# Small products of a chunked delta rule, issued in another order

## Chip, cores, metric

The kernel runs on one core of one Trainium2 chip. The metric is the device time of one execution in microseconds (us), the median over runs. Engines are named as the profile names them: PE is TensorE's matmul side, PEld its weight loads, DVE VectorE, ACT ScalarE, POOL GpSimd, SP SyncE, which issues the DMAs.

## What is computed

A token sequence `x` of 256 tokens of 1024 channels goes through two hybrid layers (latent attention, gated convolution, sparse attention, feed-forward), then through a second block with two branches, differential attention and a gated delta rule in both directions over time, and at last through a mixture of 16384 small experts. Only the delta rule matters here. The reference states it as a recursion over tokens: a state S of 64 x 64 for each of 16 heads and for each direction, which every token decays, corrects along its key and adds to, and which is read with the token's r. It first runs over 256 context tokens, which leave only their state, and from that state over the 256 tokens of `x`, which also give outputs.

The kernel computes the same by chunks of 32 tokens: within a chunk the products of all pairs and a triangular inverse, between chunks a recursion over 8 chunks.

## The kernel before

**Staging.** The program has three parts: the hybrid layers (0 to about 1050 us in the profile), the second block (to about 2070 us), and the experts. In the second block weight products (lines 325 to 327 and 343 to 345, f32 split in two parts of one pass each), the attention's heads and the delta rule are separate streams that share the engines. The delta rule is worked off in four rounds: source 0 (context) for heads 0 to 7, then for heads 8 to 15, source 1 (`x`) for both. A round is a call of `wkv_front`, all that needs no state, and one of `wkv_back`, the recursion over chunks and, for source 1, the outputs. The large tiles of a round ("w8", nine buffers) are needed by the next one, so that a front can do only part of its work before the recursion ahead of it has ended.

**Order.** Dependences and the order in which each engine's queue is filled come from a planner that lays out the whole traced program against a simulated time (line 1920). The delta rule is traced under high priority (lines 1546 and 1550), so the planner puts other streams' work into its gaps. On the chip each engine works its queue in order. The planner treats a tile's reads and writes by their place in the free dimension: a product into other partitions of the same columns of a bank still waits for an earlier read of them. Banks: the stream of the fronts has two that rotate, the stream of the recursions three.

**Names.** `d` is the direction (0 forward, 1 backward), `m` one of four channel tiles, `b` one of the two heads in it (rows 0 to 63 or 64 to 127), `q` one of four pairs of chunks, `c2` the chunk in it. In step n of the recursion direction 0 works on chunk n and direction 1 on chunk 7 - n.

- Line 1270, in `wkv_front`: pair products of every chunk, 64 rows by 64 columns of the array. Rows by `b`, columns by `c2`. Lines 1272 and 1274 mask them on DVE (two multiplies per bank without outputs, four with).
- Lines 1290 to 1294: the triangular inverse, 31 steps of a multiply and a subtraction on DVE. Lines 1315 and 1322 work beside it.
- Line 1344, in `wkv_back`: WR times the state S. Rows by `b`, columns by `c2` (with source 0 only 32 columns). Line 1347 adds the result to U on DVE, line 1353 copies outputs on ACT.
- Line 1359: the inverse ML times U, 32 rows by 32 columns of the array, both by `c2`. Line 1360 evicts it (ACT).
- Line 1369: KT times U, rows by `c2`, columns by `b`. Lines 1370 and 1371 update S on DVE.
- Line 1384: the outputs, 64 rows by `c2`, 32 columns by the chunk in its token tile, `g`. Lines 1385 and 1386 sum them up on DVE.
- Line 996 belongs to another stream: 128 rows, four strips of 32 columns in turn. Line 260 is the helper that evicts on ACT; lines 263, 266 and 269 are the helpers for multiply, add and subtract.

Of the kernel before, what the change touches and what calls it, by code (L numbers as in the profile page):

```python
# [19 lines left out]
T = 256  # L20
# [6 lines left out]
# ---------------------------------------------------------------- host layout  # L27
# [56 lines left out]
def constants():  # L84
    p = Pack()
    pos = np.arange(256)
    c, s = _rope_tab(pos, 16, 32)
    p.add("mla_c", _tok(c)), p.add("mla_s", _tok(s))
    c, s = _rope_tab(pos, 8, 16)
# [6 lines left out]
    # second block  # L96
# [5 lines left out]
    h = np.arange(128) // 64  # L102
# [91 lines left out]
# ---------------------------------------------------------------- device  # L194
class Kern:
# [17 lines left out]
    # tiles  # L213
# [22 lines left out]
    @contextmanager  # L236
    def stream(self, sfx, single=False):
        """tiles of small operands and banks of their own for one of the streams that run side by side"""
        old = self.sfx, self.single
        self.sfx, self.single = sfx, single  # L240
        yield
        self.sfx, self.single = old
# [7 lines left out]
    # engines  # L250
# [20 lines left out]
    def rsqrt(self, x, n):  # L271
        """x: tile AP [p, n]; returns 1/sqrt(x), bit estimate and three Newton steps."""
# [14 lines left out]
    # weights  # L287
# [21 lines left out]
    def pieces(self, name, piece=None):  # L309
        """Yields (h, l) pieces of a weight unit."""  # L310
# [9 lines left out]
    def mmA(self, ps, wh, wl, xh, xl, first, last):  # L320
        """ps[m, t] += W^T X; wh/wl [128, nk, 128], xh/xl [128, nk, t]"""
# [7 lines left out]
    @contextmanager  # L329
    def behind(self, ins):  # L330
        """queues products behind an earlier one"""
        if ins is None:
            yield
        else:
            with self.tc.issue_after(ins.ins):
                yield

    def mmB(self, ps, xh, xl, wh, wl, first, last):
        """ps[t, n] += X^T W for one token tile; xh/xl [128, nk, 128], wh/wl [128, nk, n]"""
# [7 lines left out]
    def linB_unit(self, name, hh, hl, n):  # L347
        """token-major product with a K=1024 unit of n columns; one bank [128, 2 token tiles, n]"""
# [12 lines left out]
    def linA_unit(self, name, hh, hl, nk):  # L361
        """channel-major product with a unit [m, k, 128]; yields banks of two m-tiles"""
# [16 lines left out]
    def pairs_split(self, h, lo, ps, scale=None, bias=None):  # L379
        """h + lo = ps (times a per-partition scale)"""  # L380
# [13 lines left out]
    def normT(self, x, g, hh, hl, eps=1e-6, bias=None, spare="", hold=False):  # L394
        """hh + hl = (rms_norm(x) * g [+ bias])^T, x: two token tiles [128, 1024]; with hold the next weights are split behind it"""
# [43 lines left out]
    def softmax(self, ps, p, G, scale, gate=None):  # L439
        """p = softmax(scale * ps) over the last axis (times gate); ps, p [128, G, n] views"""  # L440
# [16 lines left out]
    def rope_rows(self, v, c, s, half, tmp):  # L457
        """v [..., 2*half] in place; c = [cos, cos], s = [-sin, sin] broadcast to the shape of v"""
# [5 lines left out]
    # ------------------------------------------------------------ hybrid layer  # L464
    def layer(self, l, pool):
# [19 lines left out]
        # ---- MLA projections  # L485
# [36 lines left out]
        with self.stream("n", True):  # L522
            # ---- compression
# [68 lines left out]
        # ---- gated convolution  # L592
# [42 lines left out]
        with self.stream("t"):  # L635
            # per-head norms
# [28 lines left out]
        # ---- NSA projections  # L665
# [31 lines left out]
        with self.stream("t"):  # L697
            # attention
# [38 lines left out]
        with self.stream("n"):  # L737
            # ---- compressed branch
# [37 lines left out]
            # ---- selected and window branches  # L776
# [103 lines left out]
        # ---- feed-forward  # L880
# [30 lines left out]
    def gates(self, l, pool, i, hh, hl, park=False):  # L911
        """tanh of half the mixing logits of branch i, two tiles [128, 4, T]"""
# [13 lines left out]
    def merge(self, l, pool, P, M, i, name, TGs, xh, xl):  # L926
        """M (+)= 2 sigmoid(gate i) * (X @ W_o [+ b])"""
# [17 lines left out]
    def in_turn(self, late):  # L945
        """products (t, n, k, operands) in the order of their banks"""
# [7 lines left out]
    def linB_acc(self, name, pw, xh, xl, first, last):  # L954
        """pw[t] [128, 2, 512] += X^T W over two k-tiles of a [2, 1024] unit; the last unit ends one bank after the other"""
# [16 lines left out]
    # ------------------------------------------------------------ second block  # L972
# [5 lines left out]
    def mods_stream(self):  # L978
        """modT [128, 48, 2]: the 6 modulation vectors, channel-major, for x and for ctx; yields after each weight unit"""
# [33 lines left out]
    def mod_rows(self, i, w, out):  # L1013
        """out: two halves [128, 512]: modulation vector i on every partition"""
# [14 lines left out]
    def da_front(self, pool, a, name, hh, hl):  # L1029
        """head maps to a [128, 2, 16, 64]; returns their norms"""  # L1030
# [12 lines left out]
    def da_tail(self, pool, front, g, rope, dst, off):  # L1043
        """normed (and roped) head maps, transposed, to dst [128, 8, *] from column off; yields after every two heads"""
# [29 lines left out]
    def rope_tables(self, pool, g, name):  # L1074
        """[128, (cos, sin), 2 token tiles, 64]: the axial angles with the head gains g [128, 64] folded in"""
# [16 lines left out]
    def shifted(self, out, ps, mt):  # L1092
        """centred shift of one channel tile, psum [128, T] -> out"""
# [6 lines left out]
    def ctx_norm(self, pool, tag):  # L1100
        """the normalised context, in the place of the last layer's activations"""
# [7 lines left out]
    def w_proj(self, pool, src, hh, hl):  # L1109
        """(tanh(wd) | ad) and sigmoid(gd)"""  # L1110
# [14 lines left out]
    def z_proj(self, pool, src, hh, hl, zd):  # L1125
        """shifted r, k, v to zd [128, 24, T]"""
# [19 lines left out]
    def wkv_front(self, pool, src, hf, zd, wa, own=False):  # L1146
        """gated delta rule over one source and 8 heads, both directions, chunks of 32: all that does not need the state.
        Rows of packed token tiles are (c4, t32); rows of stacked ones (c2, (k, b), t32) or (c2, (v, u), t32)."""
# [10 lines left out]
        # normalised keys  # L1159
# [19 lines left out]
        # values by token, packed and in the rows of the stacked tiles  # L1179
# [8 lines left out]
        # bonus  # L1188
# [10 lines left out]
        # decays and products, channel-major  # L1199
# [11 lines left out]
        for d in range(2):  # L1211
            # log decays, chunks of 33 with a leading zero; L: their sums
# [31 lines left out]
            # K: half the inverse decay; b = 2 a kk, k = 2 k_eff  # L1244
# [12 lines left out]
        # pair products by (k, b) in rows, the b rows of the strict ones transposed for the first direction  # L1257
# [4 lines left out]
        for q in range(4):  # L1262
            for b in range(2):
                Q = slice(64 * b, 64 * b + 64)
# [659 lines left out]
```

## Time and profile before

| | us |
|---|---|
| median of three runs | 2906.81 |
| lowest, highest | 2900.73, 2912.28 |
| span of the profiled execution | 2922.4 |
| PE busy in it | 2777.9 (95%) |
| DVE busy | 1985.9 (68%) |
| ACT busy | 1428.5 (49%) |

The profile gives the profiled execution's span, from its first to its last instruction; what lies around it is not told apart. The span is 15.6 us above the median of the runs. In the timeline a row merges neighbours of one line: its length runs from the first start to the last end, and the number in brackets is the idle time of that engine before it, with what ended it. Matmuls are pipelined, so a row's length holds the last product's latency once.

### The profile page before, as it was taken

Reading aid. Unit: us, or ns where it says so; the run is one execution under the profiler, and the core shown is the slowest. Engines: PE = TensorE matmul, PEld = TensorE weight load, DVE = VectorE, ACT = ScalarE, POOL = GpSimd, SP = SyncE. Lnnn points to the kernel's source line nnn. Section 1 sums busy time; section 2 is a strip of 40 time slices with the busy share of each in tenths; the row PEclk is TensorE's granted clock in tenths of the full one; section 3 lists DMA queues with packets and bytes.
Section 4 is the critical chain, followed back from the end, with each engine's and each line's share of the span. In section 5 each row is a group of like instructions: output and inputs, shape, how many; then the busy total and the mean of one; then the engine's idle time right before and its main releaser. Section 6 shows DMA issues by size and latency. Waiting matters only on the chain. (4 is left out here: it accounts for less than half of the span.)

```text
span 2922.4 us, 55072 instructions
## 1 busy us (share of the span) xinstructions
PE 2777.9 (95%) x21880; PEld 2448.0 (84%) x21880; DVE 1985.9 (68%) x4104; ACT 1428.5 (49%) x2417; POOL 13.3 (0%) x36
## 2 busy tenths in 40 slices
PE   7999999999999998999898899898989999999999
PEld 7986688898678997889787678798989998888887
DVE  5986555698665577886868665347787775666665
ACT  4554444555454456564444544225435654444444
POOL 0000000000000000000000000000000000000000
PEclk9999999999899998999888765579999999999999
DMA  5543755454375554544434212045455345666665
GB/s 184 174 143 132 277 196 187 162 177 142 112 249 188 186 192 131 167 145 120 149 120 136 82 34 81 1 137 195 153 174 167 118 139 182 218 214 216 214 214 186
DMA packets 214738, 467.16 MB, mean 160 GB/s; under 512 B 53072, under 2 KB 86608, under 8 KB 213968
## 3 DMA queue, kind: packets, MB, share of 16 engines
q1 hardware_dynamic: 214480, 463.64, 48.5%
q8 instruction: 172, 2.82, 0.4%
q14 instruction: 86, 0.70, 0.1%
HBM read 425.54 MB, written 38.01 MB: 159 GB/s over the span
## 5 line engine op out<-in xcount | busy, mean ns | idle before, releaser
L304 ACT ACTIVATE wh<-raw 128x1024 fp32r<-128x1024 f32 (+2 forms) x726 | 643.6, 890 | 727.5 <-PE a L326 340.3
L269 DVE TENSOR_TENSOR wl<-raw,wh 128x1024 fp32r<-128x1024 f32 (+2 forms) x726 | 732.8, 1012 | 384.6 <-ACT wh L304 374.3
L325 PE MATMUL a<-hh,wh 128*128 128x256 f32 x2784 | 796.6, 286 | 17.6 <-ACT wh L304 10.4
L327 PE MATMUL a<-hh,wl 128*128 128x256 f32 x2784 | 796.6, 287 | 6.8 <-DVE wl L269 6.6
L326 PE MATMUL a<-hl,wh 128*128 128x256 f32 x2784 | 795.1, 286 | 2.5 <-DVE hl L269 1.8
L325 PEld LDWEIGHTS a<-hh,wh 128*128 128x128 f32 x2784 | 534.2, 192 | 29.3 <-ACT wh L304 13.2
L327 PEld LDWEIGHTS a<-hh,wl 128*128 128x128 f32 x2784 | 532.8, 192 | 17.1 <-DVE wl L269 10.9
L326 PEld LDWEIGHTS a<-hl,wh 128*128 128x128 f32 x2784 | 532.9, 191 | 9.7 <-DVE hl L269 2.6
L344 PE MATMUL a<-wl,hh 128*128 128x256 f32 (+2 forms) x640 | 196.4, 307 | 13.6 <-DVE wl L269 13.2
L344 PE MATMUL b<-wl,ah 128*128 128x512 f32 x512 | 200.9, 392 | 0.0
L343 PE MATMUL a<-wh,hh 128*128 128x256 f32 (+2 forms) x640 | 193.1, 306 | 7.5 <-DVE hl L387 6.7
L343 PE MATMUL b<-wh,ah 128*128 128x512 f32 x512 | 191.0, 393 | 3.6 <-issue 3.6
L345 PE MATMUL b<-wh,al 128*128 128x512 f32 x512 | 192.0, 392 | 0.0
L345 PE MATMUL a<-wh,hl 128*128 128x256 f32 (+2 forms) x640 | 191.9, 301 | 0.0
L260 ACT ACTIVATE w<-a 32x512 f32<-32x512 f32 (+1 forms) x168 | 99.4, 592 | 140.2 <-PE a L1359 68.4
L344 PEld LDWEIGHTS a<-wl,hh 128*128 128x128 f32 x640 | 127.3, 199 | 26.2 <-DVE wl L269 16.8
L343 PEld LDWEIGHTS a<-wh,hh 128*128 128x128 f32 x640 | 127.7, 200 | 14.7 <-DVE hl L387 7.3
L1769 ACT ACTIVATE ah<-pact 128x256 fp32r<-128x256 f32 x128 | 52.7, 412 | 169.1 <-PE b L344 163.5
L345 PEld LDWEIGHTS a<-wh,hl 128*128 128x128 f32 x640 | 127.0, 198 | 3.8 <-issue 0.8
L269 DVE TENSOR_TENSOR wl<-rawv,wh 128x1024 fp32r<-128x1024 f32 x84 | 101.8, 1223 | 38.7 <-ACT wh L304 38.6
L827 DVE SCALAR_TENSOR_TENSOR z<-U,pk,z 128x256 f32<-128x256 f32 x240 | 114.6, 477 | 0.8
L269 DVE TENSOR_TENSOR al<-pact,ah 128x256 fp32r<-128x256 f32 x128 | 53.0, 422 | 90.8 <-ACT ah L1769 90.8
(515 smaller groups left out, 4606.4 us busy)
## 6 DMA issues: line engine op xcount, KB each, us to landing
raw<-in_flat SPq DMA_DIRECT2D x266, 512.0 KB, 3.7
raw<-in_peer SPq DMA_DIRECT2D x172, 512.0 KB, 3.9
raw<-in_flat SPq DMA_DIRECT2D x276, 256.0 KB, 3.4
rawv<-in_peer SPq DMA_DIRECT2D x84, 512.0 KB, 4.3
TG<-in_flat SPq DMA_DIRECT2D x28, 512.0 KB, 5.8
qk<-in_flat SPq DMA_DIRECT2D x24, 512.0 KB, 5.2
parked<-act SPq DMA_DIRECT2D x89, 128.0 KB, 1.9
pact<-parked SPq DMA_DIRECT2D x89, 128.0 KB, 4.0
```

The costliest lines, as they stand in the source:

```text
L260: nc.scalar.activation(out, in_, AF.Copy, scale=1.0 if scale is None else scale)
L269: self.nc.vector.tensor_tensor(out, a, b, op=ALU.subtract)
L304: self.nc.scalar.activation(h, src, AF.Copy)
L325: mm(ps, wh[:, k], xh[:, k], start=first and k == 0, stop=False)
L326: mm(ps, wh[:, k], xl[:, k], start=False, stop=False)
L327: mm(ps, wl[:, k], xh[:, k], start=False, stop=last and k == nk - 1)
L343: mm(ps, xh[:, k], wh[:, k], start=first and k == 0, stop=False)
L344: mm(ps, xh[:, k], wl[:, k], start=False, stop=False)
L345: self.last = mm(ps, xl[:, k], wh[:, k], start=False, stop=last and k == nk - 1)
L827: nc.vector.scalar_tensor_tensor(cv[:, c], U[:, c, k_:k_ + T], wd[:, k_:k_ + 1], cv[:, c], op0=ALU.mult, op1=ALU.add)
L1769: nc.scalar.activation(ah, act, AF.Copy)
```

## The change

Five loops are put in another order. No operation is added or taken away and no operand changes; banks that were taken one by one are taken together (`pq`, `pk`).

- Line 1270: both banks of a chunk pair are taken first, `b` goes inside `m`, the masks of both banks come after all products of the pair.
- Line 1344: `m` goes outermost, then `d`, then `b`; the sums of both directions come after all products.
- Line 1359: `m`, `b`, then `d` innermost; both evictions come after all products.
- Line 1369: the same as line 1344, with one bank per direction; the updates of S follow.
- Line 1384: `g` goes from outermost to innermost.

The rest of the diff takes out comments and docstrings. Its core:

```diff
         for q in range(4):
-            for b in range(2):
-                Q = slice(64 * b, 64 * b + 64)
-                ps = self.bank()[:, 0:256 * (1 + src)].rearrange("p (d m x s) -> p d m x s", d=2, m=4, s=32)
-                for d in range(2):
-                    for m in range(4):
+            pq = [self.bank()[:, 0:256 * (1 + src)].rearrange("p (d m x s) -> p d m x s", d=2, m=4, s=32) for b in range(2)]
+            for d in range(2):
+                for m in range(4):
+                    for b in range(2):
+                        Q = slice(64 * b, 64 * b + 64)
                         for c2 in range(2):
...
+            for b in range(2):
                 for d in range(2):
-                    self.mul(ML[:, d, q, b], ps[:, d, :, src], strict[:, 1 - d].unsqueeze(1).to_broadcast([128, 4, 32]))
+                    self.mul(ML[:, d, q, b], pq[b][:, d, :, src], strict[:, 1 - d].unsqueeze(1).to_broadcast([128, 4, 32]))
...
-            for d, q, c2 in dc:
-                rows = slice(64 * c2, 64 * c2 + 64) if src else slice(64 * c2 + 32, 64 * c2 + 64)
-                for m in range(4):
+
+            for m in range(4):
+                for d, q, c2 in dc:
+                    rows = slice(64 * c2, 64 * c2 + 64) if src else slice(64 * c2 + 32, 64 * c2 + 64)
                     for b in range(2):
                         Q = slice(64 * b, 64 * b + 64)
                         mm(pp[b][rows, m], WR[d][Q, m, 2 * q + c2].rearrange("p x s -> p (x s)"), S[Q, d, m], start=True, stop=True)
+            for d, q, c2 in dc:
                 u = slice(64 * c2 + 32, 64 * c2 + 64)
...
+            for m in range(4):
+                for b in range(2):
+                    for d, q, c2 in dc:
+                        u = slice(64 * c2 + 32, 64 * c2 + 64)
+                        mm(pt[u, m, b], ML[u, d, q, b, m], U64[d][u, q, m, b], start=True, stop=True)
             for d, q, c2 in dc:
                 u = slice(64 * c2 + 32, 64 * c2 + 64)
-                for m in range(4):
-                    for b in range(2):
-                        mm(pt[u, m, b], ML[u, d, q, b, m], U64[d][u, q, m, b], start=True, stop=True)
                 self.evac(UV[d][u, q], pt[u].rearrange("p m b i -> p m (b i)"))
...
-            for d, q, c2 in dc:
-                R = slice(64 * c2, 64 * c2 + 64)
-                ps = self.bank()[:, 0:256].rearrange("p (m i) -> p m i", m=4)
-                for m in range(4):
+            pk = [self.bank()[:, 0:256].rearrange("p (m i) -> p m i", m=4) for d in range(2)]
+            for m in range(4):
+                for d, q, c2 in dc:
+                    R = slice(64 * c2, 64 * c2 + 64)
                     for b in range(2):
                         Q = slice(64 * b, 64 * b + 64)
-                        mm(ps[Q, m], KT[d][R, m, q, Q], U64[d][R, q, m, b], start=True, stop=True)
-                self.add(S[:, d], S[:, d], ps)
+                        mm(pk[d][Q, m], KT[d][R, m, q, Q], U64[d][R, q, m, b], start=True, stop=True)
+            for d, q, c2 in dc:
+                self.add(S[:, d], S[:, d], pk[d])
                 self.mul(S[:, d], S[:, d], PC[:, d, :, 2 * q + c2].unsqueeze(2).to_broadcast([128, 4, 64]))
...
-            for g in range(4):
-                q, c2 = divmod(4 * t + g, 2)
-                R = slice(64 * c2, 64 * c2 + 64)
-                for m in range(4):
-                    for b in range(2):
-                        for d in range(2):
+            for m in range(4):
+                for b in range(2):
+                    for d in range(2):
+                        for g in range(4):
+                            q, c2 = divmod(4 * t + g, 2)
+                            R = slice(64 * c2, 64 * c2 + 64)
                             mm(ps[32 * g:32 * g + 32, m, b], NK[R, d, q, b, m], U64[d][R, q, m, b], start=d == 0, stop=d == 1)
```

## Rows read from the trace of the kernel before

**Rows 1.** The page: span, busy time by engine, granted clock in 40 slices.

```profile
span 2922.4 us, 55072 instructions
...
PE 2777.9 (95%) x21880; PEld 2448.0 (84%) x21880; DVE 1985.9 (68%) x4104; ACT 1428.5 (49%) x2417; POOL 13.3 (0%) x36
...
PEclk9999999999899998999888765579999999999999
```

**Rows 2.** Stages: length; busy (count) of PE, PEld, DVE, ACT, POOL; PEclk, DMA share, GB/s.

```profile
1212.00:1345.00 133.00, 130.92 (x1475) 118.01 (x1473) 100.28 (x195) 72.80 (x132) 1.21 (x3) 0.97 0.48 148
1420.00:1545.00 125.00, 115.93 (x1254) 101.04 (x1253) 88.89 (x193) 58.63 (x102) 1.21 (x3) 0.84 0.40 126
1617.00:1737.00 120.00, 108.28 (x962) 79.10 (x964) 77.63 (x161) 68.79 (x164) 1.11 (x2) 0.74 0.19 58
1757.00:1817.00 60.00, 58.90 (x571) 50.83 (x570) 34.16 (x98) 20.53 (x41) 0.00 (x0) 0.50 0.22 70
1817.00:1925.00 108.00, 96.00 (x1015) 85.62 (x1015) 34.43 (x77) 29.63 (x70) 0.00 (x0) 0.55 0.07 16
```

**Rows 3.** PE by line; the first gives line 1359's count, the others start, length, count.

```profile
L1359 PE MATMUL a<-w,w x1024: 211/214/312, 1211.8 to 1898.8; 32*32 32x64 f32 x171
...
1442.62 1.08 PE L1359 MATMUL a<-w,w 32*32 32x64 f32 x16
...
1449.42 0.64 PE L1344 MATMUL a<-S,w 64*32 64x64 f32 x16
...
1447.75 0.68 PE L1369 MATMUL a<-w,w 64*64 64x64 f32 x16
...
1566.27 1.08 PE L1322 MATMUL a<-w,w 32*32 32x64 f32 x32 [0.72 <-ACT w L260]
...
1594.31 1.92 PE L1322 MATMUL a<-w,w 32*32 32x64 f32 x32
...
300.91 1.05 PE L996 MATMUL m<-TG,cs 128*32 128x512 f32 x2
...
317.48 1.06 PE L996 MATMUL m<-qk,cs 128*32 128x512 f32 x8
```

**Rows 4.** Timeline of the fourth recursion: one lone step, then its outputs.

```profile
1838.67 1.12 PE L1344 MATMUL a<-S,hh 64*64 64x64 f32 x16 [0.33 <-DVE S L263]
1839.79 0.75 DVE L266 TENSOR_TENSOR w<-w,a 32x256 f32<-32x256 f32 x2 [0.47 <-PE a L1344]
...
1840.26 1.11 PE L1344 MATMUL a<-S,hl 64*64 64x64 f32 x8 [0.47 <-DVE w L266]
...
1844.42 0.59 ACT L260 ACTIVATE w<-a 32x512 f32<-32x512 f32 x1 [1.79 <-PE a L1359]
...
1845.06 1.91 PE L1359 MATMUL a<-w,w 32*32 32x64 f32 x16 [0.68 <-ACT w L260]
...
1846.90 1.86 PE L1369 MATMUL a<-w,w 64*64 64x64 f32 x32
...
1848.07 0.42 DVE L266 TENSOR_TENSOR S<-S,a 128x256 f32<-128x256 f32 x1 [4.84 <-PE a L1369]
...
1849.09 1.12 PE L1344 MATMUL a<-S,hh 64*64 64x64 f32 x16 [0.33 <-DVE S L263]
1849.31 0.43 DVE L263 TENSOR_TENSOR S<-S,PC 128x256 f32<-128x256 f32 x1
...
1900.09 24.36 PE L1384 MATMUL a<-w,w 64*32 64x64 f32 x254
```

**Rows 5.** Timeline: one chunk pair of line 1270 and its masks, third front.

```profile
1551.08 1.91 PE L1270 MATMUL a<-w,w 64*64 64x64 f32 x64
1552.28 1.67 DVE L263 TENSOR_TENSOR w<-a,consts 128x128 f32<-128x128 f32 x8 [0.68 <-PE a L1270]
```

**Rows 6.** Timeline of DVE in the last inverse: the two sums of outputs.

```profile
1778.74 0.69 DVE L266 TENSOR_TENSOR w<-w,a 128x512 f32<-128x512 f32 x1 [7.80 <-PE a L1384]
...
1798.09 0.69 DVE L266 TENSOR_TENSOR w<-w,a 128x512 f32<-128x512 f32 x1 [9.18 <-PE a L1384]
```

More of the change, by code (lines that the diff above doesn't have):

```diff
@@ L1262, in wkv_front @@
         for q in range(4):
-            for b in range(2):
-                Q = slice(64 * b, 64 * b + 64)
-                ps = self.bank()[:, 0:256 * (1 + src)].rearrange("p (d m x s) -> p d m x s", d=2, m=4, s=32)
-                for d in range(2):
-                    for m in range(4):
+            pq = [self.bank()[:, 0:256 * (1 + src)].rearrange("p (d m x s) -> p d m x s", d=2, m=4, s=32) for b in range(2)]
[3 more added lines that the diff above has]
+                        Q = slice(64 * b, 64 * b + 64)
                         for c2 in range(2):
                             rhs = WR[d][Q, m, 2 * q + c2].rearrange("p x s -> p (x s)")
-                            mm(ps[64 * c2:64 * c2 + 64, d, m].rearrange("p x s -> p (x s)"), KB[d][Q, m, 2 * q + c2].rearrange("p x s -> p (x s)"), rhs, start=True, stop=True)
+                            mm(pq[b][64 * c2:64 * c2 + 64, d, m].rearrange("p x s -> p (x s)"), KB[d][Q, m, 2 * q + c2].rearrange("p x s -> p (x s)"), rhs, start=True, stop=True)
+            for b in range(2):
                 for d in range(2):
-                    self.mul(ML[:, d, q, b], ps[:, d, :, src], strict[:, 1 - d].unsqueeze(1).to_broadcast([128, 4, 32]))
+                    self.mul(ML[:, d, q, b], pq[b][:, d, :, src], strict[:, 1 - d].unsqueeze(1).to_broadcast([128, 4, 32]))
                     if src:
-                        self.mul(NK[:, d, q, b], ps[:, d, :, 0], incl[:, d].unsqueeze(1).to_broadcast([128, 4, 32]))
+                        self.mul(NK[:, d, q, b], pq[b][:, d, :, 0], incl[:, d].unsqueeze(1).to_broadcast([128, 4, 32]))
         blk = lambda a: a.rearrange("p q b m s -> p (q b m) s")
```

## Prediction

> **What bounds the kernel now.** The page comes first: TensorE (PE) is busy for 95% of a span of 2922.4 us, VectorE (DVE) for 68%, and the granted clock sags in one stretch, slices 19 to 26, some 1390 to 1970 us [rows 1]. A busy PE is not yet a useful PE, so the next view is the table of busy time by stage over the delta rule's stretch [rows 2]. `wkv_back` runs four times. The first three recursions lie at about 1212 to 1345, 1420 to 1545 and 1617 to 1737 us, among weight products of other streams: PE is busy 130.9 of 133, 115.9 of 125 and 108.3 of 120 us. The fourth, 1817 to 1925 us, runs alone, at 0.55 of the clock: PE says 96 of 108 us, with DVE and ScalarE (ACT) at 34 and 30. What follows the fourth needs its output, so every microsecond off the chain front, recursion, front, recursion comes off the end. I therefore read the small products on that chain.
>
> The timeline of PE alone shows how they run [rows 3]. An f32 product leaves two records here: the code calls line 1359 4 x 8 x 16 = 512 times and the trace has 1024. Records are what I count. Sixteen records of line 1359, all in one 32x32 corner of the array, take 1.08 us, so (1.08 - 0.21) / 15 = 58 ns each; 32 of line 1322, which has the same shape but alternates between two corners, also take 1.08 us: 28 ns each. At half clock (1.2 of 2.4 GHz) 32 of line 1322 take 1.92 us [rows 3], 16 of line 1359 1.91 us [rows 4]. Lines 1344 and 1369 alternate between two halves already: 16 in 0.64 and 0.68 us, 28 and 31 ns. Line 996 goes round four column strips: eight records take 1.06 us, as long as two in one strip (1.05 us). So products in different parts of the array overlap, two tiles at twice and four strips at four times the rate of one.
>
> **The change, part by part.**
>
> *Line 1359 (two corners instead of one).* The two directions always sit in opposite halves (n and 7 - n have different parity), so the 32 records of a step become what line 1322 is: 0.93 us instead of 1.85 at full clock.
>
> *Lines 1344 and 1369 (four quadrants instead of two halves).* Per step 32 records each, 0.90 + 0.99 us. A round over row halves and column halves together is not in the trace by itself. Bounds: no gain (two halves were the limit) and half again, 0.45 + 0.50 us. I take the half, since line 996 is the nearest row. A step thus saves 1.85 + 1.89 - 0.93 - 0.95 = 1.86 us at full clock, 8 steps 14.9; divided by the clocks 0.97, 0.84 and 0.74 of the three mixed recursions that is 15.4, 17.7 and 20.1, together 53 us of PE.
>
> *Line 1270 (four quadrants, two banks at once).* A chunk pair of 64 records takes 1.91 us at full clock [rows 5], 27 ns each; 1024 records, halved, save 13.8 us at full clock and 27.6 at half; the four places lie between, so 20.
>
> *How much of this 73 us is time.* In the first recursion PE waited for nearly nothing (2.1 of 133 us not busy), in the second and third 9 and 12 us. The fill is planned into the gaps of the chain and stays, so the freed time is time unless a wait appears. Bounds: a fifth (15 us, waits on DVE and ACT take the rest) and all of it (73). I take 0.6, **44 us**.
>
> *Line 1384 in the fourth recursion.* 254 records in one 64x32 tile at a time hold PE for 24.36 us, 96 ns each on end, with nothing else running [rows 4]. With g innermost, neighbours go round four tiles: 7 us with four at once, 13 with two. Saved **17** (bounds 11 and 17.5).
>
> *Line 1384 after the third recursion.* It lies beside the triangular inverse of the last front, which is a DVE chain. There the chain stops twice, 7.80 and 9.18 us, because the sum of outputs queued on DVE between two inverse steps waits for line 1384 [rows 6]. PE is busy 58.9 of 60 us at half clock, with 256 x 96 ns, some 25 us, of line 1384 among it. Cut to a quarter, PE is 18 us further on, more than the 17.0 us of stops; cut to half, 12 us. So **17** (bounds 10 and 17). Next late there is the inverse itself; the last attention rounds are on the same PE queue and move up with it.
>
> *The chain in the fourth recursion.* One step is 10.42 us (1838.67 to 1849.09) [rows 4]. Now: line 1344 of direction 0; line 1344 of direction 1 waits for DVE's sums, which read the same bank; line 1359 of direction 0, its eviction by ACT (0.59 us), only then line 1359 of direction 1 (same bank again), its eviction, line 1369, and add and multiply on the state S for both directions. After, at the same clock: line 1344 in eight rounds of 107 ns, line 1359's (1.91 - 0.31) / 15 with a record of 312 ns at most [rows 3], plus 0.3 = 1.15; four sums, two of which take 0.75 us, = 1.5; line 1359, 16 pairs, 1.92; two evictions 1.2; line 1369 1.15; four steps on S, 1848.07 to 1849.74, 1.7. Sum 8.6, with hand-overs 8.75. What is lost is counted in it: line 1344 may start today when S of direction 0 is ready, 0.65 us before the other; now its third product needs both. Seven periods save 7 x 1.67 = **12** (bounds 0, if four quadrants run no faster than two, since lines 1344 and 1369 then give 0.85 us each back, and 16).
>
> *Evictions, Y copies (line 1353), the count of banks.* Unchanged in number; the three banks of the recursion are handed out in the same order. The Y copies queue on ACT ahead of the evictions while line 1359 runs its 1.92 us: hidden. Nothing.
>
> *What it adds.* Line 1270 used to fill one bank while DVE masked the other; now both fill, then both drain, and the next pair's third product stands at the head of PE's queue until DVE has done all 8 masks (1.67 us; four, half of that, with no outputs), with the weight products behind it. Today DVE's eight begin 1.20 us into the pair [rows 5]. Cost between 0 (weight products are planned in between, as between two pairs now) and 16 pairs x 1.3 = 21 us; it is inside the 0.6.
>
> Sum: 44 + 17 + 17 + 12 = 90 us. The profiled span is 2922.4 us, 15.6 above the median of 2906.81 (three runs, 2900.73 to 2912.28). 2906.8 - 90 = **2817 us**.
>
> **Rivals.**
>
> A, *more than two tiles bring nothing*, because the array takes no more at once or because the planner pulls neighbours apart (it cut line 1344 into 16, 8 and 8 [rows 4]). Then lines 1344, 1369 and 1270 stay, line 1359 saves 7.4 us a back at full clock, 26 over the three, of which 0.6 is 16; line 1384 11 and 10; the lone chain 0: 37 us, 2870. Against it speaks line 996.
>
> B, *the mixed recursions give nothing*: the chain there is set by waits, or PE, idling a little more, is granted less clock (it was granted 0.97 in the first, 0.74 in the third). Only 17 + 17 + 12 is left: 2861. Against: 2.1 us not busy in the first.
>
> C, *row tiles that share a bank don't overlap.* Line 1359 (both directions in one bank) then stays single and line 1384 goes in two groups. Saved: lines 1344, 1369 and 1270, 47 us of which 0.6 is 28; line 1384 11 and 10; lone chain 12 less 1.7 us for each of seven single line 1359s, 0: 49 us, 2858. Rows 3 speak against it: line 1322 writes both its corners into one bank and gets 28 ns. The Trainium skill (TensorEngine Tiling (Array Packing), Gotcha 1: PSUM Pressure) says that different row tiles cannot access the same PSUM bank simultaneously; by it the time would be C's, and line 1322's rows disagree with it where the outputs lie in different partitions.
>
> D, *slower: lockstep.* Both directions now wait for each other. If the planner leaves no weight products between, PE stands bare in each mixed step for four sums (1.5 us) and four steps on S (1.7 us), and in each pair for 1.3. The gains are 44 + 46; 16 x 1.3 = 21 for pairs plus 24 mixed steps of x us eat them from x = 2.9, nearly all of the 3.2; at 3.2, with the freed 44 lost as well, the result is 2906.8 - 46 + 21 + 77 = 2959. For it: PE's queue is in order. Against: the fill stands between these groups now, and its amount does not change.
>
> **How the numbers follow.** Forecast 0.66, A 0.12, B 0.11, C 0.04, D 0.07. The forecast's own bounds: all of the 73, 17.5, 17 and 16 make 123 us, 2783; a fifth of the 73 with the rest as forecast makes 61 us, 2846. The planner works on the changed order as a whole, which can give more than PE's own time, so the low end goes to 2772; the high end takes in A: 2772 to 2872. Half a per cent, 14.5 us, is what a measurement of this kernel can tell from no change. All but D are faster by more than that; D, from x = 2.9 to 3.2, is within it for 0.02 and slower for 0.05: faster 0.93, same 0.02, slower 0.05.
>
> **What will show it.** Right: 32 records of line 1359 in about 1.1 us at full clock; lines 1344 and 1369, 32 in some 0.7 us; line 1384 of the fourth recursion in about 7 us; no stop over 2 us in the last inverse; lone steps of some 8.8 us. Wrong: line 1344 still 28 ns per record (A), mixed recursions as long as now (B), line 1359 at 58 ns (C), waits of PE on DVE at lines 1270, 1344 and 1369 of microseconds each (D).

## The result, and the profile after

The changed kernel takes 2840.1 us (median of four runs, 2832.75 to 2845.82) against 2907.58 us (four runs, 2900.73 to 2912.28) beside it: a ratio of 0.9753, interval 0.9726 to 0.9781, 67 us less. The forecast was 2817 us and its range 2772 to 2872 us: faster as foretold, by 67 us where the sum said 90.

The lines of the change moved down by a few: 1344 is now 1346, 1359 is 1362, 1369 is 1374, 1384 is 1390, 1322 is 1323; 1270 stays. In the experiments lines are called by their numbers before. The page of the changed kernel, the rows that answer [rows 1]:

```profile
span 2837.1 us, 55078 instructions
...
PE 2637.1 (93%) x21880; PEld 2314.7 (82%) x21880; DVE 1977.8 (70%) x4104; ACT 1424.6 (50%) x2417; POOL 13.1 (0%) x36
...
PEclk9999999999999998999897766599999999999999
```

The two profiled spans differ by 85.3 us, 18 more than the medians. 19 of it lie ahead of the change: the first transfer of the second block starts at 1050.4 us before and at 1031.4 after, though DVE and ACT work in the same order up to there. From there to the end the two traces differ by 66.3 us, as the medians do within 1 us. (Where a run's time and span are both on record the span is some 2 us below the time; by that the execution traced before took about 2924 us, more than each of the four runs beside it.) So lengths of stages are compared, not positions. Stages of the changed kernel: the three mixed recursions, the last inverse, the lone recursion and its outputs (columns as in [rows 2]):

```profile
1193.00:1322.00 129.00, 123.34 (x1583) 111.38 (x1584) 103.63 (x205) 74.29 (x137) 1.20 (x3) 0.97 0.52 163
1397.00:1505.00 108.00, 96.03 (x1216) 83.29 (x1216) 80.83 (x178) 57.42 (x101) 1.20 (x3) 0.91 0.44 138
1584.00:1707.00 123.00, 103.03 (x1056) 71.73 (x1060) 82.55 (x181) 71.79 (x175) 1.10 (x2) 0.68 0.23 70
1718.00:1764.00 46.00, 25.56 (x442) 20.37 (x436) 35.73 (x101) 23.68 (x52) 0.00 (x0) 0.73 0.21 57
1769.00:1832.00 63.00, 45.73 (x704) 35.07 (x702) 26.89 (x61) 20.54 (x45) 0.00 (x0) 0.50 0.03 5
1832.00:1863.00 31.00, 29.81 (x446) 28.19 (x444) 22.46 (x42) 12.79 (x22) 0.00 (x0) 0.91 0.43 137
```

From the first to the last record of line 1359 a recursion took 135.7, 118.7, 137.6 and 77.3 us before; now 128.4, 107.7, 122.4 and 63.2. The terms of the sum, each between the same two events of both traces (the mixed part runs from a load of the first front, line 1153, until DVE has masked the last pair; the inverse's transfer is the one that writes the inverse out, `dout`; the outputs end with their store):

| term | foretold | measured |
|---|---|---|
| mixed part (first front to the last pair of line 1270) | 44 | 688.4 to 671.5: 16.9 |
| last pair to the inverse's transfer | 17 | 62.5 to 46.0: 16.5 |
| lone recursion | 12 | 77.3 to 63.2: 14.1 |
| its outputs | 17 | 49.4 to 30.5: 18.9 |
| sum | 90 | 66.4 |

Three terms came within some 2 us of what was worked out. One, the mixed part, is 27 us short and makes the error. The same stretch as one row of windows, before and then after:

```profile
1065.00:1753.00 688.00, 631.62 (x6966) 547.29 (x6964) 508.31 (x1177) 367.88 (x714) 4.72 (x11) 0.86 0.42 127
```

```profile
1046.00:1717.00 671.00, 585.83 (x7155) 502.24 (x7154) 504.24 (x1185) 369.48 (x728) 4.71 (x11) 0.86 0.44 133
```

PE is busy 46 us less, but the stretch is only 17 us shorter: PE stands idle 85 us in it (671.00 - 585.83), 56 before. What PE waits for there, the longest of the changed kernel (total, times, longest):

```profile
PE a L344 <- DVE wl L269: 11.4, 5, 5.6
PE a L1069 <- DVE x L266: 11.2, 3, 5.3
PE a L1362 <- DVE w L266: 9.8, 12, 3.8
PE a L1362 <- DMA w<-dout: 7.7, 3, 6.2
PE a L1346 <- DVE S L263: 7.1, 5, 3.4
PE a L1270 <- DVE w L263: 5.8, 5, 1.9
```

and of the kernel before:

```profile
PE a L344 <- DVE wl L269: 9.5, 9, 2.5
PE a L1069 <- DVE x L266: 4.5, 1, 4.5
...
PE a L1270 <- DVE w L263: 3.6, 2, 3.2
PE a L1359 <- DVE w L266: 3.3, 3, 1.4
```

No single wait took the 29 us. They are spread over the sums that line 1362 needs (9.8 against 3.3 us), the state (7.1 us, none before), the transfer behind the inverse (7.7 against 2.4 us) and work of the other streams. The granted clock is 0.86 in both rows, so it is not the clock that took them.

**The overlap itself** is there. Timeline of PE at full clock (1.00 in each of these rows), first recursion and third front of the changed kernel:

```profile
1202.26 1.08 PE L1362 MATMUL a<-w,w 32*32 32x64 f32 x30
1206.41 0.70 PE L1374 MATMUL a<-w,w 64*64 64x64 f32 x32
1211.61 0.65 PE L1346 MATMUL a<-S,w 64*32 64x64 f32 x32
...
1520.42 1.32 PE L1270 MATMUL a<-w,w 64*64 64x64 f32 x64
```

In the time in which 16 records of lines 1359, 1344 and 1369 ran [rows 3], 30 to 32 run now; 64 of line 1270 take 1.32 us and not 1.91 [rows 5]. A step of the lone recursion, the rows that answer [rows 4]:

```profile
1785.63 0.48 PE L1346 MATMUL a<-S,hh 64*64 64x64 f32 x4 [0.46 <-DVE S L263]
...
1786.33 0.37 PE L1346 MATMUL a<-S,hl 64*64 64x64 f32 x2 [0.22 <-DVE S L263]
...
1787.48 1.77 DVE L266 TENSOR_TENSOR w<-w,a 32x256 f32<-32x256 f32 x4 [1.20 <-PE a L1346]
...
1787.95 3.06 PE L1362 MATMUL a<-w,w 32*32 32x64 f32 x32 [0.50 <-DVE w L266]
...
1791.04 1.20 ACT L260 ACTIVATE w<-a 32x512 f32<-32x512 f32 x2 [0.94 <-PE a L1362]
...
1791.68 1.73 PE L1374 MATMUL a<-w,w 64*64 64x64 f32 x32 [0.68 <-ACT w L260]
...
1793.88 0.48 PE L1346 MATMUL a<-S,hh 64*64 64x64 f32 x4 [0.46 <-DVE S L263]
```

A step is 8.25 us (1785.63 to 1793.88), 10.42 before. Line 1362 takes 3.06 us in it because its first records wait for DVE's four sums one after the other (0.45 us each); from the last sum on its two corners run in pairs. And the outputs, first a stretch of those of the third recursion at half clock, then those of the lone one, and DVE's two sums in the last inverse, which answer [rows 4] and [rows 6]:

```profile
1710.07 1.50 PE L1390 MATMUL a<-w,w 64*32 64x64 f32 x46
...
1837.08 3.19 PE L1390 MATMUL a<-w,w 64*32 64x64 f32 x189
1841.46 0.98 PE L1390 MATMUL a<-w,w 64*32 64x64 f32 x53 [1.19 <-issue]
```

```profile
1718.60 0.65 DVE L266 TENSOR_TENSOR w<-w,a 128x512 f32<-128x512 f32 x1
...
1732.17 0.68 DVE L266 TENSOR_TENSOR w<-w,a 128x512 f32<-128x512 f32 x1
```

The sums that waited 7.80 and 9.18 us wait for nothing now.

### The profile page after: what moved, and what is told of

The parts are those of the page before. It is cut to its first block, busy times and chain, and to the rows that moved or that the text cites. A ratio compares the mean times of both kernels' runs of the same rounds, so it can differ in the third digit from the quotient of the medians.

```text
span 2837.1 us, 55078 instructions
## 1 busy us (share of the span) xinstructions
PE 2637.1 (93%) x21880; PEld 2314.7 (82%) x21880; DVE 1977.8 (70%) x4104; ACT 1424.6 (50%) x2417; POOL 13.1 (0%) x36
```

## The experiments

Theory at the start: small products are paid as the prediction has them, and in the mixed recursions PE is the bound, so that what the small products leave is filled by weight products or lost to waits. The rivals, by run: single lines or the tie of the directions carry or cost the gain; the fill only rides along; VectorE has become the bound.

**Line 1384 alone.**

```diff
-            for g in range(4):
...
+            for m in range(4):
+                for b in range(2):
+                    for d in range(2):
+                        for g in range(4):
```

> Kernel before with line 1384 alone in the new order. Theory (the end moves only by what sits on the chain): the two stops of the last inverse go (7.8 and 9.2 us before) and the outputs of the fourth recursion shrink from 24.4 to some 5 to 7 us: 33 to 36 us less than before. Rival (the last inverse is held by other work on DVE, not by line 1384): only the fourth recursion's part, 17 to 19 us.

Measured 0.9885 (0.9839 to 0.9931), 2876.34 against 2910.73 us. Windows of the last inverse and of the lone outputs:

```profile
1749.00:1799.00 50.00, 35.73 (x631) 29.18 (x631) 38.27 (x108) 24.97 (x55) 0.00 (x0) 0.77 0.37 101
1877.00:1904.00 27.00, 26.79 (x420) 25.73 (x419) 19.01 (x37) 11.24 (x19) 0.00 (x0) 0.92 0.47 148
```

Before, from the end of one recursion to the start of the next and from the last record of line 1359 to the store of the outputs, 66.5 and 49.4 us: half of the whole gain comes from this loop, and its two terms hold by themselves (34 us less, 33 to 36 expected).

**Line 1359 alone, line 1344 alone, line 1369 alone**, each in its new order in the kernel before:

```diff
+            for m in range(4):
+                for b in range(2):
+                    for d, q, c2 in dc:
+                        u = slice(64 * c2 + 32, 64 * c2 + 64)
+                        mm(pt[u, m, b], ML[u, d, q, b, m], U64[d][u, q, m, b], start=True, stop=True)
```

```diff
-            for d, q, c2 in dc:
-                rows = ...
-                for m in range(4):
+            for m in range(4):
+                for d, q, c2 in dc:
+                    rows = ...
```

```diff
+            pk = [self.bank()[:, 0:256].rearrange("p (m i) -> p m i", m=4) for d in range(2)]
+            for m in range(4):
+                for d, q, c2 in dc:
```

> Kernel before with line 1359 alone in the new order. It frees some 22 us of PE in the three mixed recursions and halves line 1359 in the lone one. Theory (of PE time freed in mixed recursions only about a quarter becomes time): about 6 us there and 8 in the lone recursion, 12 to 16 us less. Rival (mixed recursions are bound by PE, and it was the new waits of the other lines that ate the gain): 15 to 20 us there and 8 in the lone one, 23 to 28 us less.

> Kernel before with line 1344 alone in the new order. Theory: the lone recursion loses the wait between the directions, 1.3 us a step less 0.65 for the later start, some 5 us over the lone recursion; in the mixed ones PE now waits at its head for four sums in a row, and 18 us of freed PE time give 0 to 5 us: 5 to 10 us less in all. Rival (PE-bound): 15 to 20 us less.

> Kernel before with line 1369 alone in the new order. In the changed kernel's lone recursion 32 records of this line still take 1.73 us against 1.86, direction after direction. Theory (the planner pulls the directions apart, since one eviction ends before the other): between 3 us less and 3 us more. Rival (four quadrants, half of its PE time back): 8 to 12 us less.

Measured 0.9999 (0.9973 to 1.0026), 1.0025 (0.9994 to 1.0056) and 1.0012 (0.9982 to 1.0043): no gain from any, against a gain foretold for the first two; for line 1369 the theory had it. From the first front to the program's end the traces take 1860 us before and 1861, 1860 and 1860 us with one line. Mixed part of the runs with line 1359 and with line 1344:

```profile
1061.00:1759.00 698.00, 624.82 (x7034) 536.42 (x7033) 509.69 (x1196) 374.70 (x746) 4.75 (x11) 0.85 0.42 128
```

```profile
1050.00:1754.00 704.00, 631.85 (x7031) 550.64 (x7029) 511.99 (x1196) 377.27 (x747) 4.76 (x11) 0.85 0.42 127
```

The lone recursion fell as it should with line 1359 (77.3 to 69.8 us; with line 1344 by under 2 us, where 5 were expected), but the mixed part grew from 688 to 698 and 704 us, with PE idle 73 and 72 us in place of 56. Counted in the traces, the first two recursions hold more weight products (838 + 496 and 780 + 567 records of other lines, 716 + 455 before) and the inverses between fewer. With line 1369 alone these counts are those of before, the mixed part is 693 us with PE idle 57, and in the lone recursion its directions do not alternate: 32 records still take 1.87 us.

**Lines 1344 and 1359 together; the change without line 1270; lines 1344, 1359 and 1384 alone of the five.** The edits are the hunks above put together, and for the second the old loop put back:

```diff
-            pq = [...]
-            for d in range(2):
-                for m in range(4):
-                    for b in range(2):
+            for b in range(2):
+                ps = ...
+                for d in range(2):
+                    for m in range(4):
```

> The kernel before with two loops in the new order: the reads of the state (line 1344) and the products with the inverse (line 1359). Alone they gave 1.0025 and 0.9999 of the time before. If parts add (rival), together 1.002, some +7 us. My theory: alone, the tie of the two directions at one line makes a planned step of the mixed recursions longer, and the planner puts more weight products into them (716 records of fill in the first recursion became 780 and 838); with both lines tied the step is tied only once more, so the fill of the first recursion stays near 780 to 840 while the small products take 6.8 us less in each of three mixed recursions. The whole change less lines 1384 and 1369 gave about -34 us: if these two lines carry it, the time is 0.987 to 0.990 of before (-30 to -37 us); if line 1270 is needed, it is 0.995 to 1.002.

> The changed kernel with the loop of line 1270 (pair products) put back in its old order, everything else of the change kept. My theory (the planner fills freed TensorE time of the recursions with weight products, so the mixed part follows the fill and not the small products): the 128 pairs of a source stand in the front ends, where 15 us of TensorE at most are freed, and in the changed kernel's trace the stretch from the end of the third recursion to the last pair grew from nothing to 10.7 us; the time stays within 6 us of the changed kernel (2834 to 2846 us). Rival (each freed microsecond of line 1270 counts as the prediction had it, 0.6 of it): 15 x 0.6 = 9 us or more slower than the changed kernel, 2849 us or above. Rival 2 (holding two banks at a time for the pairs costs more than the overlap gives): 5 to 11 us faster, 2829 to 2835 us.

> The kernel before with three of the five loops in the new order: lines 1344, 1359 and 1384; lines 1270 and 1369 as before. Theory: these three carry the whole gain. Line 1384 alone gave 0.9885 and lines 1344 and 1359 together 0.9864 of the time before; their sum is 0.975, so 0.972 to 0.978 (the whole change: 0.9753). Rival: lines 1270 and 1369, which gave nothing alone or when left out, matter once the others are in: 0.980 or above.

Measured 0.9864 (0.9834 to 0.9895), 0.9741 (0.9704 to 0.9777) and 0.9752 (0.9708 to 0.9796). Mixed parts, in this order:

```profile
1053.00:1714.00 661.00, 587.82 (x7016) 510.08 (x7014) 502.06 (x1172) 362.89 (x707) 4.75 (x11) 0.86 0.44 133
```

```profile
1049.00:1712.00 663.00, 577.89 (x7023) 499.00 (x7022) 504.01 (x1178) 365.42 (x715) 4.71 (x11) 0.87 0.44 132
```

```profile
1051.00:1721.00 670.00, 597.94 (x7051) 518.63 (x7050) 502.44 (x1173) 363.12 (x707) 4.74 (x11) 0.84 0.43 131
```

How far a single trace can be read is seen in the first and the third of these kernels: DVE and ACT work the same order in both up to the end of the third recursion, yet their first recursions differ by 6 us and their granted clocks by 0.05:

```profile
1200.00:1329.00 129.00, 125.30 (x1663) 112.57 (x1664) 103.89 (x209) 70.83 (x131) 1.21 (x3) 0.97 0.50 155
```

```profile
1198.00:1333.00 135.00, 131.19 (x1666) 117.94 (x1666) 104.39 (x209) 71.18 (x131) 1.20 (x3) 0.92 0.49 150
```

The mixed parts differ by 9 us (661 and 670). The kernel before and the one with line 1384 alone also share this order; their first recursions take 135 and 141 us (0.97 and 0.93), their mixed parts 688 us both. So a difference of less than some 6 us in one recursion, or 10 us in the mixed part, is no reading.

All three times are as the theories had them, the first a little under its 0.987. Two lines that give nothing alone give 40 us together (some 28 in the mixed part, 14 in the lone recursion, which is as short as in the whole change). Three of the five lines make the whole gain; lines 1270 and 1369, and with them the banks that are taken together, add nothing that these runs can tell (their intervals are 11 to 13 us wide to either side). Parts do not add up for lines 1344 and 1359, but they do for that pair and line 1384 (0.9864 and 0.9885 make 0.975). The expected fill of 780 to 840 records in the first recursion did not come, though: it is 706. PE's idle time is 73 us with either line and 73 with both (661.00 - 587.82). So it looks as if tying the two directions costs some 17 us of waits once, and two lines' products pay for it where one line's do not. The other traces fit in part: PE idles 59 us with line 1384 alone and 72 with three lines, but 85 in the changed kernel and without line 1270, the two that have line 1369 beside the other ties. That reading is argued from the rows, no run has a tie without the faster products, and why the weight products were placed otherwise with one line is open.

**Fill held back.** The second half of the second source's shifted r, k, v products (weight products, 288) queued behind the first recursion, in the changed kernel; then half as many (144) in the kernel with line 1359 alone and, as its control, in the kernel before:

```diff
-        self.z_proj(pool, 1, hh, hl, zx)
+        self.z_proj(pool, 1, hh, hl, zx, mark)
...
+                    with self.behind(after if f"{n}{i}" in ("zv3", "zr2", "zr3") else None):
```

> The changed kernel, with the second half of the shifted r, k, v products of the second source (288 weight products, about 33 us of TensorE) queued behind the last line-1359 product of the first recursion; they are needed only by the last front end. If the mixed recursions are bound by TensorE through the fill (my theory): the first recursion falls from 128 us to 95 to 105 us, the held products reappear in the next inverse (where TensorE idled 16 us) and in the second recursion; the total falls by 5 to 20 us, to 2820 to 2835 us. Rival (the chain of a step bounds the recursions, fill only rides along): the first recursion stays at 125 to 130 us and the total grows by what the moved products cost later, 0 to +25 us.

> The kernel before with line 1359 alone in the new order (1.0000 of before by itself, first recursion 143.9 us with 838 weight products in it, against 135.7 us with 716), and three of the weight units of the second source's shifted products (144 of these products) queued behind the last line-1359 product of the first recursion. Theory: line 1359 alone gave nothing because more weight products were placed into the recursion, where TensorE is the bound, and fewer into the inverse behind it, where it idles 16 us. So the first recursion falls by 144 x 0.128 = 18 us (107.6 us for 838), to 122 to 130 us, the inverse behind grows by less than 12 us, and the total comes to 0.994 to 0.998 of before. Rival: a step whose two directions are tied is longer on the chip by itself, and the products only ride along: first recursion 138 us or more, total 1.000 or above.

> The kernel before, unchanged but for the same three weight units queued behind the last line-1359 product of the first recursion. Control for the run with line 1359. Theory: the first recursion falls by 144 x 0.132 = 19 us to 115 to 122 us (94.3 us for 716), but the inverse behind it has only 8 us of idle TensorE, so it grows by 8 to 14 us and the rest goes into the second recursion: total 0.996 to 1.001 of before. If this run gains as much as the one with line 1359, holding products back is a gain by itself and says nothing on why line 1359 alone gave none. Rival (fill only rides along): first recursion 132 us or more.

Measured 0.9730 (0.9693 to 0.9767), 0.9999 (0.9976 to 1.0022) and 1.0005 (0.9975 to 1.0034). The first recursion of each:

```profile
1202.00:1302.00 100.00, 79.33 (x1133) 67.28 (x1131) 69.00 (x142) 44.00 (x82) 1.20 (x3) 0.74 0.32 101
```

```profile
1206.00:1327.00 121.00, 106.96 (x1391) 94.29 (x1392) 84.00 (x173) 52.68 (x100) 1.21 (x3) 0.80 0.36 113
```

```profile
1204.00:1337.00 133.00, 124.73 (x1413) 109.07 (x1412) 85.62 (x176) 54.90 (x101) 1.20 (x3) 0.76 0.37 111
```

In the first two the recursion shrinks as the theory says, 128 to 100 and 144 to 121 us: there PE with its fill sets the length. In the control it misses: 135.7 to 133 us and not 115 to 122. There the granted clock is 0.76 and not 0.97, lines 1344, 1359 and 1369 take 49 us instead of 36, and 128 more records of line 1270 stand in the stretch (10.0 us, 3.5 before). In none does the total follow: with line 1359 alone the mixed part is 697 us, as without holding, and in the changed kernel the 0.9730 cannot be told from 0.9753. There the mixed part is 650 us, 21 less than in the changed kernel, but from its end to the end of the lone recursion it takes 131 us where the changed kernel takes 115. Work moved between these stages comes back in the next ones, so the length of one stage says little about the sum, and the placing of the fill is not shown to be what made single lines worthless.

**VectorE.** Two runs: the second direction's eviction behind line 1359 on VectorE; and a fourth of the weight splits taken from VectorE to ScalarE (this kernel leaves out their subtraction, the low part is a plain copy), both in the changed kernel:

```diff
+                if d:
+                    nc.vector.tensor_copy(UV[d][u, q], pt[u].rearrange("p m b i -> p m (b i)"))
+                else:
+                    self.evac(...)
```

```diff
+            if getattr(self, "light", False) and self.nth % 4 == 0:
+                self.nc.scalar.activation(lo, src, AF.Copy)
+            else:
+                self.sub(lo, src, h.bitcast(F32))
```

> The changed kernel with the second direction's eviction behind line 1362 (line 1365) on VectorE instead of ScalarE, so that the evictions of the two directions run beside each other instead of one behind the other. In the lone fourth recursion a step's two evictions then end together and the products of line 1374 of both directions may alternate: a step falls from 8.25 to 7.4 to 7.8 us (an eviction of 0.6 us less on the chain, one VectorE operation of about 0.3 us more), the recursion by 4 to 6 us. In the mixed recursions VectorE gets 24 more operations of about 0.3 us, 7 us. If the chain decides there: -10 us in all, 2830 us. If TensorE through the fill decides there (my theory): the mixed part within 5 us, the total -2 to -8 us, 2832 to 2838 us. Rival (VectorE, 70% busy, is late in the inverses and front ends): slower by 0 to 7 us.

> The changed kernel with every fourth of the weight splits of the second block, up to the merge behind the fourth recursion, made otherwise: the low part is a copy of the weights by ScalarE in place of VectorE's subtraction (line 269), so the product with the low part is left wrong. In the mixed part (first front end to last pair) that takes some 45 of 183 subtractions of 0.69 us, 31 us, off VectorE and puts 45 copies of 0.63 us, 28 us, on ScalarE, which is half idle there. Theory, after the run that put 23 copies of 0.69 us on VectorE and made the mixed part 17 us longer: with TensorE's work cut, VectorE sets the pace of the mixed part, so the freed TensorE time went into waits for VectorE. Then the mixed part falls by 15 to 30 us and the total to 2810 to 2825 us (0.965 to 0.970 of before). Rival (TensorE with its weight products still sets it): mixed part and total within 6 us of the changed kernel. Rival 2 (ScalarE becomes late with evictions and high parts): slower by up to 15 us.

Measured 0.9799 (0.9770 to 0.9828) and 0.9779 (0.9753 to 0.9806). Both miss. The first has a lone step of 8.24 us, no shorter; timeline of its evictions:

```profile
1815.44 0.59 ACT L260 ACTIVATE w<-a 32x512 f32<-32x512 f32 x1 [0.94 <-PE a L1362]
1816.06 0.70 DVE L1366 COPY w<-a 32x512 f32<-32x512 f32 x1 [2.41 <-ACT w L260]
```

VectorE's copy starts only when ScalarE's has ended: the two still run one behind the other, although on two engines. In the trace the copy waits for the semaphore that ScalarE's eviction raises: the program orders the two, so evictions side by side stay untested. The mixed parts, eviction first:

```profile
1054.00:1742.00 688.00, 603.18 (x7049) 518.53 (x7049) 524.68 (x1219) 361.63 (x723) 4.74 (x11) 0.84 0.43 130
```

```profile
1046.00:1709.00 663.00, 586.30 (x7149) 502.25 (x7147) 479.05 (x1141) 389.38 (x770) 4.75 (x11) 0.86 0.44 133
```

With 20 us more of VectorE the mixed part is 17 us longer; with 25 us less it is 8 us shorter, which is within the scatter of single traces (and this one is of the fastest of five executions, 17 us under their median), and the time is no better than the changed kernel's. So less work for VectorE alone gives nothing that these runs can tell, and the first of the two runs is no proof that VectorE sets the pace.

## Why the prediction was right, and where it was off

- **Unit prices.** Right. Lines 1359, 1344 and 1369 run 30 to 32 records where 16 ran at full clock. The bound "no gain from four quadrants", and with it A, fell for line 1344. For line 1369 A holds in the lone recursion: the planner pulled its directions apart, 32 records take 1.73 us where 1.15 was foretold and 1.86 measured before.
- **One bank, two row tiles (C).** Fell once more: the 30 records of line 1362 at 1202.26 go to both corners of one bank. The Trainium skill (TensorEngine Tiling (Array Packing), Gotcha 1: PSUM Pressure) would have them one by one; this trace disagrees where the outputs lie in different partitions.
- **Outputs of the fourth recursion.** 18.9 us for 17. The tiles gave what was foretold (26 ns a record at half clock, see the last section), and luck helped: line 1384 ran at half clock before (0.50 from 1900 to 1924 us); now weight products run ahead of it and the granted clock is 0.90 from 1837 to 1841 us, which the prediction did not have.
- **The stops in the last inverse.** 16.5 us for 17, and in the first experiment, with line 1384 alone, again 16.6 (66.5 to 49.9 us between the recursions).
- **The lone chain.** 14.1 us for 12. Steps are 8.25 us, 8.75 were foretold, and line 1346's third product does wait for S of the second direction, as the prediction said (0.22 us at 1786.33). Inside the step two errors cancel in part: line 1374 is 0.6 us over its price, but line 1362 starts under the sums and not behind them.
- **The mixed part** is the term that was mis-sized: "I take 0.6, 44 us". 16.9 us came, 0.23 of 73, with some 10 us of scatter on a single trace. Two parts: the small products freed 57 us of PE in this trace, not 73 (199.3 to 142.5 us of record spacing, lines 1322 and 1384 counted in); and of the 57, 29 became idle time of PE and some 11 went to other products (weight products take some 3 us more, and 32 more attention records stand in the stretch, some 7 us), so 17 were left. Where the 57 fall short is line 1270: lines 1344, 1359 and 1369 freed 51 us of the 53, line 1270 10.6 of the 20, and 149 records of line 1384 that moved into the stretch took 3 back. The reason for the 0.6, "the freed time is time unless a wait appears", named the right danger; the waits that appeared were not priced. The lower bound, a fifth (15 us), was the better value here; with lines 1344 and 1359 alone the stretch got some 28 us shorter for 41 freed. Within the three recursions, from the first to the last record of line 1359, the 0.6 is not far off: their own lines freed 47 us there and they got 33.5 us shorter, some of it because pairs of line 1270 left the third (12.6 to 2.1 us). What the prediction did not price is what follows them: the inverses between grew by 3.6 us, and the masks of the last pair now end 10.7 us behind the third recursion, where they ended 1.9 us ahead of its end before. So the last front end did not move up with the recursion beside it.
- **Line 1270** was priced at 20 us of PE, 12 us of the 44. Without it the time is the same (0.9741 against 0.9753, each known to some 10 us), and three lines without it make the whole gain: nothing shows its share.
- **D, lockstep.** Its mechanism is real but small: in the mixed part the waits of lines 1362 and 1346 for VectorE's sums and for S are 16.9 us (9.8 + 7.1), where lines 1359 and 1344 had 5.8 (3.3 + 2.5), and one line tied alone makes the mixed part 10 to 16 us longer, as much as the scatter of one trace or somewhat more. With the products of two lines freed, it does not decide.

What stays open: what exactly turns the freed time into idle time in the mixed part. Neither the fill's place nor VectorE alone is shown to account for it, and every edit reorders the stretch.

## What to carry to other kernels

Neighbouring small products should sit in different rows and columns of the array. Where PE runs alone or another engine stands waiting for it, the gain was the worked-out one; in a stretch where PE shares the pace with VectorE, transfers and a planned fill, it was less: here from nothing (one line) over 0.3 (the whole change) to some half or two thirds (lines 1344 and 1359, with and without line 1384) of the freed time, each from one trace. Try such reorderings of a chain together as well as one by one: each alone may cost the tie and not pay for it. Before a few microseconds of one stage are read as an effect, see how much two traces of the same order differ there.

## What was not expected of the hardware

Tiles that differ in row half and column strip at once, which no row before showed, gave all that was foretold: at half clock 46 records of line 1384 take 1.50 us, (1.50 - 0.31) / 45 = 26 ns each, where one tile took 96 ns; in the lone recursion, also at half clock, line 1346 runs rounds of four records in some 107 ns, their starts 7 ns apart. In the last outputs 189 records take 3.19 us, 17 ns each, at a granted clock of 0.90.

The granted clock of the first recursion fell in all three runs that held weight products back: with 275 fewer records of other lines in it from 0.97 to 0.76 in the kernel before, where lines 1344, 1359 and 1369 took 49 us instead of 36; from 0.97 to 0.74 in the changed kernel; and from 1.00 to 0.80 with line 1359 alone. PE was busy 94% of the time even so in the first of them. In these traces fill beside small products kept PE at the higher of its two levels for more of the time, so taking it out made the small ones longer; two kernels of one order differed by 0.05 at most.
